# 320 columns of room and a start on 256 bytes for the tiles that move through TensorE

## The chip, the core and the metric

One NeuronCore of a Trainium2 chip runs the whole program. The metric is device microseconds from launch to end, the median of several runs. TensorE multiplies, VectorE (DVE), ScalarE (ACT) and GpSimd (POOL) do the elementwise work, SyncE (SP) issues the DMAs that bring weights from HBM.

## What is computed

One inference step of a two-layer decoder over 256 prompt tokens and 8 x 4 sample tokens, 288 tokens in all, model width 2048, feed-forward width 5632, float32. Cut to what matters:

```python
def trunk(x, ...):
    for l in range(2):
        h = rmsnorm(x, norm_mix[l])
        if l % 2 == 0:  y_tok, q_mem, ... = delta_mixer(h, ...)  # h @ w_in_delta, conv, gated delta rule
        else:           y_tok, q_mem, ... = pool_mixer(h, ...)   # h @ w_in_pool, windowed means, grouped w
        y_mem = cross_attn(q_mem, mem_k[l], mem_v[l])            # keys, values: rmsnorm(mem) @ w_mem_kv
        x = x + concat([y_tok, y_mem]) @ w_out[l]
        x = x + (silu(gate) * up) @ w_down[l]                    # gate, up = rmsnorm(x) @ w_gate_up[l]
    return rmsnorm(x, norm_final), states...
```

## The kernel before

Activations lie feature-major: a tile holds 128 features of all 288 tokens, 288 float32 columns or 1,152 bytes of each partition. Nearly all of the arithmetic is in the projections, and all projections go through one generator, `gemm_steps` (lines 143 to 166). It takes up to four 128-column blocks of a weight matrix, gives each block j a PSUM bank (`acc`), and walks the contraction in steps of `ks` blocks of 128 rows (two of them where four blocks are computed at once). For each step `wchunk` (line 103) fetches the weights by one DMA into one of three `wraw` tiles and splits them in two halves: ScalarE rounds them to float32r (`whi`, line 118) and VectorE takes the remainder (`wlo`, line 119). The activations have been split in the same way by `split` (line 168) into a hi tile and a lo tile. For each row block k and each column block j three matmuls follow, here called a triple:

```python
nc.tensor.matmul(pv, wh, xh, start=st, stop=False)      # line 161
nc.tensor.matmul(pv, wh, xl, start=False, stop=False)   # line 162
nc.tensor.matmul(pv, wl, xh, start=False, stop=en)      # line 163
```

The weight half is the stationary operand (128 x 128), the activation half is the moving operand (128 x 288). There are 5,860 triples in the program. Within one step j runs inside k, so four triples in a row, 12 matmuls, move the same pair of activation tiles; the last step of a projection runs k inside j.

The moving tiles come from three rotating sets. `at()` (line 65) gives one of `NA = 47` tiles named `a`, which serve all projections except two kinds; `bt()` (line 1350) gives tiles named `b` to the feed-forward stages (60 and 50 of them), which hold the hidden blocks that `w_down` multiplies, but for the first seven of each half, whose pairs are `a` tiles (line 1367); `dk()` (line 1448) gives 12 tiles to the small grouped product of the pooling mixer (36 triples).

Where these tiles lie follows from the order of the pools. At the bottom of each partition 16,384 bytes are set aside for descriptors of DMAs generated by software (the program constructor's default). Then come the constants, the pool `small` (line 50), the pool `act` with the 47 `a` tiles, the pool `wts` with `wraw`, `whi` and `wlo`, and the stage pools. The layout of the program before has:

- first `a` tile at byte 34,944 = 136 x 256 + 128, one every 1,152 = 4.5 x 256 bytes
- `whi` and `wlo` tiles at multiples of 2,048 bytes from byte 101,376 = 396 x 256; their 128-column slices at multiples of 512 bytes from there
- first `b` tile of the second feed-forward stage at byte 136,192 = 532 x 256, one every 1,152 bytes; the first stage's likewise on a multiple of 256
- first `dk` tile at byte 152,736 = 596 x 256 + 160, one every 1,152 bytes

So `a` and `b` tiles lie in turn on a multiple of 256 bytes and 128 bytes past one. Which of the two a hi or lo tile gets is decided by the rotation. The 16 pairs of the first feed-forward stage's input (`n1`), which all 22 of its gate and up projections move in the same order, lie as follows for row blocks 6 to 13 (start of hi, start of lo, each modulo 256):

```
k       6      7      8        9        10      11     12      13
hi, lo  0, 0   0, 0   128,128  128,128  128,0   0, 0   0,128   128,128
```

The order of the instructions on TensorE is fixed when the program is built. In the delta stage (some 100 to 800 us) the projections of the next heads are interleaved with the small matmuls of the delta rule, in the pooling stage with the cross attention; in the feed-forward stages there is nothing but triples.

Of the kernel before, what the change touches and what calls it, by code (L numbers as in the profile page):

```python
# [8 lines left out]
F32 = mybir.dt.float32  # L9
# [13 lines left out]
NT = NP + NS  # L23
NS3 = 3 * NS
# [18 lines left out]
def body(ctx: ExitStack, tc: tile.TileContext, i: dict, o: dict):  # L43
# [21 lines left out]
    def at(dt=F32):  # L65
        return apool.tile([P, NT], dt, name="a", tag="a", bufs=NA)

# [35 lines left out]
    def wchunk(pieces, nk, ncols, early=300):  # L103
        """Rows of weights, split into float32r parts: [(hi, lo)] of each 128 rows."""
        raw = wpool.tile([P, 1024], F32, name="wraw", tag="wraw", bufs=3)
        rv = raw[:, : nk * ncols].rearrange("p (k c) -> p k c", c=ncols)
        for ap, c0, w in pieces:
            nc.sync.dma_start(rv[:, :, c0 : c0 + w], ap)
        r = []
        step = 512 // ncols  # L110
        for k in range(0, nk, step):
            m = min(step, nk - k)
            n = m * ncols
            hi = wpool.tile([P, 512], F32R, name="whi", tag="whi", bufs=4)
            lo = wpool.tile([P, 512], F32R, name="wlo", tag="wlo", bufs=4)
            src = raw[:, k * ncols : k * ncols + n]
            with tc.high_priority(offset=early):
                nc.scalar.copy(hi[:, :n], src)  # L118
                nc.vector.tensor_tensor(  # L119
                    lo[:, :n], src, hi[:, :n].bitcast(F32), op=ALU.subtract  # L120
                )
            r += [
                (hi[:, j * ncols : (j + 1) * ncols], lo[:, j * ncols : (j + 1) * ncols])
                for j in range(m)
            ]
        return r
# [16 lines left out]
    def gemm_steps(w2d, cols, kt, act, on_block, ks=2, order=None, bank=None):  # L143
        """cols: [(first column, width)]; act(k) -> (hi, lo); on_block(j, psum)."""
        ncols = sum(w for _, w in cols)
        nb = ncols // P
        src = wsrc(w2d, cols)
        pss = [(bank or acc)() for _ in range(nb)]
        order = order or list(range(0, kt, ks))
        for k0 in order:  # L150
            nk = min(ks, kt - k0)
            w = wchunk(src(k0, nk), nk, ncols)
            last = k0 == order[-1]
            kj = [(k, j) for k in range(nk) for j in range(nb)]
            for k, j in sorted(kj, key=lambda t: t[1]) if last else kj:
                pv = pss[j][:, :NT]
                xh, xl = act(k0 + k)
                wh, wl = (t[:, j * P : (j + 1) * P] for t in w[k])
                st = k0 == order[0] and k == 0
                en = last and k == nk - 1  # L160
                nc.tensor.matmul(pv, wh, xh, start=st, stop=False)  # L161
                nc.tensor.matmul(pv, wh, xl, start=False, stop=False)  # L162
                nc.tensor.matmul(pv, wl, xh, start=False, stop=en)  # L163
                if en:
                    on_block(j, pv)
            yield
# [14 lines left out]
    class Norm:  # L181
        """Feature-major activations: hi/lo parts of x*w and the token sums of x^2."""
# [34 lines left out]
    def token_rstd(ss):  # L217
        """ss[token, tile]: sums of squares -> 1 / rms, [P, 3]."""
        v = small(3, "fv")
        nc.gpsimd.memset(v, 1.0)  # L220
        for r, c in ((slice(0, P), slice(0, 2)), (slice(0, NS), slice(2, 3))):
            nc.vector.tensor_scalar(v[r, c], ss[r, c], 1.0 / D, EPS, op0=ALU.mult, op1=ALU.add)
        return rsqrt(v, 3, "c3")

    def spread(r):
        """[token, tile] -> the same row of tokens on all partitions."""
        ps = aux()
        for t in range(3):
            rows = P if t < 2 else NS
            nc.tensor.matmul(  # L230
                ps[:, t * P : t * P + rows], r[:rows, t : t + 1].broadcast_to([rows, P]),
                ident[:rows, :rows], start=True, stop=True,
            )
        row = sp.tile([P, NT], F32, name="rrow", tag="rrow", bufs=1)
        nc.vector.tensor_copy(row, ps[:, :NT])
        return row

# [81 lines left out]
    with tc.tile_pool(name="mem", bufs=1) as mp:  # L319
# [50 lines left out]
        # masks: partition index j, free index c  # L370
# [18 lines left out]
        # sample tokens stand three times on the partitions: the parts of a split  # L389
        # product are then summed along one contraction  # L390
# [6 lines left out]
        # additive masks: 0 where the decay is kept, NEG elsewhere  # L397
# [4 lines left out]
        # within 32-blocks, [(block, j), c]: identity, and masks of the solved size s:  # L402
        # j in an even run of s, c in the odd run that follows
# [18 lines left out]
        # products with the states of the samples come out as rows (head, b, w|q, t)  # L422
# [17 lines left out]
        # 1 on the rows w, 0 on the rows q  # L440
# [27 lines left out]
    def attention(l, ys, g2, s4):  # L468
# [38 lines left out]
        # sample tokens: the four heads take a column tile each; a sequence's queries  # L507
        # (probabilities) stand in their own columns of a tile that is zero elsewhere
# [96 lines left out]
    W0 = i["w_in_delta"][0]  # L605
    y = [None] * 16
    with tc.tile_pool(name="delta", bufs=1) as dp:
# [4 lines left out]
        g2 = tiles("g", 2)       # 2 KB  # L612
        g1 = tiles("h", 6)       # 1 KB, keys of a unit
        gh = tiles("q", 3)       # 0.5 KB, sample tokens
        gp = tiles("u", 8)       # 2 KB, from the keys to the values of a unit
        v2 = tiles("v2", 4)      # 2 KB, values of a unit
        v1 = tiles("v1", 5)      # 1 KB, values of a unit
        ga = tiles("ag", 2)      # 2 KB, attention
        s4 = tiles("s", 4)       # 4 KB, recurrent states, cached keys and values
        pair = lambda shape, name: dp.tile(shape, F32, name=name, tag=name, bufs=2)  # L620

# [13 lines left out]
        def rates(ps):  # L635
# [24 lines left out]
            # softplus(a) = max(a, 0) + 2 atanh(e / (2 + e))  # L660
# [13 lines left out]
            # sigmoid(b) = max(e, b >= 0) / (1 + e)  # L674
# [6 lines left out]
        def decays():  # L681
            # cumulative decay within each chunk, and chunk totals
# [34 lines left out]
        # 24 columns: every fourth 128 rows in a column tile, summed with the transposition  # L717
# [16 lines left out]
        def decay(h0):  # L734
            """exp(gc_c - gc_j) for c >= j, heads h0, h0+1: [j, head, c]."""
# [50 lines left out]
        def project(fs):  # L786
            """Feature blocks of q | k | v (0..35: causal convolution and silu) and of
            z (36..47: silu), the z blocks last."""
# [83 lines left out]
        class Unit:  # L872
            """Gated delta rule for heads h0, h0+1: two prompt chunks of 128 and
            the sample tokens (8 sequences of 4)."""
# [4 lines left out]
            def bc(self, a, n=P):  # L879
                # [token, (chunk and) head], spread over head_dim  # L880
                return a.unsqueeze(len(a.shape)).broadcast_to(list(a.shape) + [P])

            def keys(self):
                # L = diag(r beta) K K' diag(r) with r = 1 / |k|, K as it comes from the
                # convolution: inverse(I + L) = diag(r beta) T diag(1 / (r beta)) with
                # T = inverse(I + K K' diag(r^2 beta) * decay); the scales of the rows
                # meet the vectors, and 1 / |q| the outputs
# [48 lines left out]
                # [j, head, (-L | attn), i]  # L936
# [43 lines left out]
                # U = transpose of inverse(I + L), by doubling the solved block; within  # L980
                # 32-blocks packed as [(block, j), chunk and head, i], samples last
# [19 lines left out]
                for s in (2, 4, 8, 16):  # L1001
# [13 lines left out]
                    # a sequence of samples is solved with the second size  # L1015
# [24 lines left out]
                # pairs of solved 32-blocks  # L1040
# [28 lines left out]
                # the two solved 64-blocks  # L1069
# [25 lines left out]
                # -w_k (feature-major)  # L1095
# [30 lines left out]
            def values(self):  # L1126
# [30 lines left out]
                # sample tokens: both products with each sequence's own state  # L1157
# [48 lines left out]
                # outputs, token-major, before the scale of q  # L1206
# [37 lines left out]
                # states  # L1244
# [77 lines left out]
    def out_proj(l, order, residual, after, ys=None):  # L1322
        """x = residual + y @ w_out; residual(g) adds to the 4 blocks of a group."""
# [24 lines left out]
    def ffn(l, nrm, fp, nbuf, after):  # L1348
        rs = None
        bt = lambda dt=F32: fp.tile([P, NT], dt, name="b", tag="b", bufs=nbuf)  # L1350
# [71 lines left out]
    W1 = i["w_in_pool"][0]  # L1422
    with tc.tile_pool(name="mix1", bufs=1) as qp:
# [4 lines left out]
        g2 = tiles("g", 6)       # 2 KB  # L1428
        ga = tiles("ag", 3)      # 2 KB, attention
        s4 = tiles("s", 5)       # 4 KB  # L1430
# [17 lines left out]
        dk = lambda: qp.tile([P, NT], F32R, name="dk", tag="dk", bufs=12)  # L1448
# [204 lines left out]
```

## Time and profile before

| what | value |
|---|---|
| median of 3 runs | 2762.17 us (2761.73 to 2766.06) |
| profiled execution, first to last instruction | 2763.6 us |
| TensorE busy with matmuls | 2720.2 us, 98% |
| VectorE, ScalarE, GpSimd busy | 58%, 46%, 12% |
| DMA engines busy (mean of 16) | 53%, 163 GB/s |
| mean granted TensorE clock | 0.995 |

The profile gives the span of the profiled execution alone; it lies 1.4 us above the median of the runs and within their spread. Matmuls are pipelined: one lasts some 295 ns from start to end in the records, and the next starts some 132 ns after it started. The number that counts is therefore the distance from start to start, not the duration.

### The profile page before, as it was taken

How to read it: one execution, taken by the hardware profiler on the slowest of the kernel's cores; microseconds unless marked ns; L12 is line 12 of the kernel's file. 1: busy time of each engine (PE TensorE's matmuls, PEld its weight loads, DVE VectorE, ACT ScalarE, POOL GpSimd, SP SyncE). 2: the span in 40 equal slices, each digit the busy share in tenths (PEclk: the TensorE clock that was granted, in tenths of full speed). 3: DMA queues.
4: the chain of work that ended last, by engine and by line, in shares of the span. 5: the costliest groups of instructions: out<-in, count | busy, mean ns of one | idle time of the engine just before them, and what ended most of it. 6: DMA issues, size and time to landing. Idle time of an engine off the chain costs nothing.

```text
span 2763.6 us, 55822 instructions
## 1 busy us (share of the span) xinstructions
PE 2720.2 (98%) x21808; PEld 2613.9 (95%) x21808; DVE 1606.1 (58%) x3240; ACT 1278.9 (46%) x2487; POOL 322.9 (12%) x671
## 2 busy tenths in 40 slices
PE   8999999999999999999999999999999999999998
PEld 6898888888999999999999988899999999999997
DVE  6657877686555554445555566766555544555544
ACT  6444545344544444344444455455444433444444
POOL 1103222231110010000010110111001000001000
PEclk9999999999999999999999999999999999999999
DMA  6544355635555555555555555655555555555554
GB/s 208 176 140 123 100 155 171 180 109 154 163 161 168 166 163 167 167 166 164 168 168 162 167 189 159 229 166 161 167 164 166 168 167 164 166 168 168 164 158 133
DMA packets 282954, 450.88 MB, mean 163 GB/s; under 512 B 18475, under 2 KB 104216, under 8 KB 282642
## 3 DMA queue, kind: packets, MB, share of 16 engines
q1 hardware_dynamic: 282690, 447.32, 52.4%
q8 instruction: 171, 2.80, 0.4%
q14 instruction: 93, 0.76, 0.1%
HBM read 434.93 MB, written 12.86 MB: 162 GB/s over the span
## 4 chain that ended last, share of the span: by engine, by line
PE 91%; DVE 3%; DMA 1%; ACT 1%; issue 1%; POOL 0%; SPq 0%; POOLq 0%; ACTq 0%; DVEq 0%
PE acc L161 27%; PE acc L163 27%; PE acc L162 27%; DVE wlo L119 1%; DMA s<-in_cache_mem_k_dram 1%; PE acc L273 1%; PE acc L274 1%; PE acc L275 1%; PE aux L523 0%; DMA memn<-in_mem_prompt_dram 0%; PE aux L569 0%; ACT whi L118 0%; PE aux L945 0%; PE aux L1011 0%; PE aux L745 0%
## 5 line engine op out<-in xcount | busy, mean ns | idle before, releaser
L119 DVE TENSOR_TENSOR wlo<-wraw,whi 128x512 fp32r<-128x512 f32 (+1 forms) x1548 | 1064.9, 694 | 996.9 <-ACT whi L118 968.6
L118 ACT CAST whi<-wraw 128x512 fp32r<-128x512 f32 (+1 forms) x1548 | 942.6, 616 | 1207.7 <-PE acc L162 1129.5
L161 PE MATMUL acc<-a,whi 128*128 128x288 f32 x4864 | 1444.6, 297 | 0.1
L163 PE MATMUL acc<-a,wlo 128*128 128x288 f32 x4864 | 1440.3, 296 | 0.9 <-DVE wlo L119 0.9
L162 PE MATMUL acc<-a,whi 128*128 128x288 f32 x4864 | 1441.2, 296 | 0.0
L162 PEld LDWEIGHTS acc<-a,whi 128*128 128x128 f32 x4864 | 916.0, 188 | 5.4 <-issue 2.9
L163 PEld LDWEIGHTS acc<-a,wlo 128*128 128x128 f32 x4864 | 914.5, 188 | 6.2 <-issue 2.4
L161 PEld LDWEIGHTS acc<-a,whi 128*128 128x128 f32 x4864 | 914.5, 188 | 5.3 <-issue 1.7
L161 PE MATMUL acc<-b,whi 128*128 128x288 f32 x960 | 283.7, 295 | 0.0
L163 PE MATMUL acc<-b,wlo 128*128 128x288 f32 x960 | 283.0, 295 | 0.0
L162 PE MATMUL acc<-b,whi 128*128 128x288 f32 x960 | 282.8, 295 | 0.0
L1362 POOL TENSOR_TENSOR b<-b,rrow 128x288 f32<-128x288 f32 x88 | 89.8, 1041 | 1266.9 <-ACT b L1361 1266.9
L162 PEld LDWEIGHTS acc<-b,whi 128*128 128x128 f32 x960 | 180.9, 188 | 0.0
L163 PEld LDWEIGHTS acc<-b,wlo 128*128 128x128 f32 x960 | 180.5, 188 | 0.0
L161 PEld LDWEIGHTS acc<-b,whi 128*128 128x128 f32 x960 | 180.4, 188 | 0.0
L196 POOL TENSOR_TENSOR ssum<-ssum,sq 128x288 f32<-128x288 f32 x60 | 56.4, 940 | 477.4 <-ACT sq L195 474.9
L275 PE MATMUL acc<-wlo,a 128*128 128x512 f32 x128 | 51.9, 405 | 0.0
L273 PE MATMUL acc<-whi,a 128*128 128x512 f32 x128 | 50.2, 414 | 1.4 <-ACT whi L118 1.1
L1360 DVE TENSOR_TENSOR b<-acc,rrow 128x288 f32<-128x288 f32 x88 | 40.1, 456 | 16.2 <-PE acc L163 16.1
L1361 ACT ACTIVATE b<-b 128x288 f32<-128x288 f32 x88 | 36.7, 441 | 26.2 <-DVE b L1360 25.9
L1366 DVE TENSOR_TENSOR b<-acc,b 128x288 f32<-128x288 f32 x88 | 40.0, 455 | 2.1 <-issue 0.3
L831 DVE SCALAR_TENSOR_TENSOR ckq<-xp,col_conv,ckq 128x312 f32<-128x312 f32 x72 | 37.4, 555 | 1.0 <-ACT ckq L829 0.9
(429 smaller groups left out, 1766.9 us busy)
## 6 DMA issues: line engine op xcount, KB each, us to landing
wraw<-in_w_gate_up_dram SPq DMA_DIRECT2D x352, 512.0 KB
wraw<-in_w_down_dram SPq DMA_DIRECT2D x176, 512.0 KB
wraw<-in_w_in_delta_dram SPq DMA_DIRECT2D x177, 256.0 KB
wraw<-in_w_out_dram SPq DMA_DIRECT2D x64, 512.0 KB
wraw<-in_w_mem_kv_dram SPq DMA_DIRECT2D x32, 512.0 KB
wraw<-in_w_in_pool_dram SPq DMA_DIRECT2D x32, 384.0 KB
wraw<-in_w_in_delta_dram SPq DMA_DIRECT2D x16, 512.0 KB
s<-in_cache_mem_k_dram SPq DMA_DIRECT2D x16, 512.0 KB
```

Source lines behind the costliest of these rows:

```text
L118: nc.scalar.copy(hi[:, :n], src)
L119: nc.vector.tensor_tensor(lo[:, :n], src, hi[:, :n].bitcast(F32), op=ALU.subtract)
L161: nc.tensor.matmul(pv, wh, xh, start=st, stop=False)
L162: nc.tensor.matmul(pv, wh, xl, start=False, stop=False)
L163: nc.tensor.matmul(pv, wl, xh, start=False, stop=en)
L196: nc.gpsimd.tensor_tensor(self.sum, self.sum, q, op=ALU.add)
L273: nc.tensor.matmul(pv, xh, w[k][0], start=st, stop=False)
L275: nc.tensor.matmul(pv, xh, w[k][1], start=False, stop=en)
L831: nc.vector.scalar_tensor_tensor(c[:, :312], xp[:, q : q + 312], convw(q, f), c[:, :312], op0=ALU.mult, op1=ALU.add,)
L1360: nc.vector.tensor_tensor(t, ps, rs, op=ALU.mult)
L1362: nc.gpsimd.tensor_tensor(t, t, rs, op=ALU.mult)
L1366: nc.vector.tensor_tensor(t, ps, t, op=ALU.mult)
```

## The change

The three sets of moving tiles get 320 columns (1,280 bytes) of room each, of which the first 288 are used; a tile of 32 columns (128 bytes) that nothing reads or writes is added to the pool `small`; the room at the bottom of the partition for software-generated DMA descriptors goes from 16,384 to 1,024 bytes. Comments and docstrings go as well. No instruction is added or removed by the text of the change, and each keeps its shape.

```diff
+NA_W = 320
     def at(dt=F32):
-        return apool.tile([P, NT], dt, name="a", tag="a", bufs=NA)
+        return apool.tile([P, NA_W], dt, name="a", tag="a", bufs=NA)[:, :NT]
+
+    sp.tile([P, 32], F32, name="fill")
...
-        bt = lambda dt=F32: fp.tile([P, NT], dt, name="b", tag="b", bufs=nbuf)
+        bt = lambda dt=F32: fp.tile([P, NA_W], dt, name="b", tag="b", bufs=nbuf)[:, :NT]
...
-        dk = lambda: qp.tile([P, NT], F32R, name="dk", tag="dk", bufs=12)
+        dk = lambda: qp.tile([P, NA_W], F32R, name="dk", tag="dk", bufs=12)[:, :NT]
...
-    nc = _bacc.Bacc("TRN2", target_bir_lowering=False, num_devices=1)
+    nc = _bacc.Bacc("TRN2", target_bir_lowering=False, num_devices=1, dynamic_dma_scratch_size=1024)
```

## Rows read from the trace of the kernel before

**Rows 1.** The page: span, and busy time of each engine.
```profile
span 2763.6 us, 55822 instructions
PE 2720.2 (98%) x21808; PEld 2613.9 (95%) x21808; DVE 1606.1 (58%) x3240; ACT 1278.9 (46%) x2487; POOL 322.9 (12%) x671
```

**Rows 2.** The page: chain that ended last, shares by engine.
```profile
PE 91%; DVE 3%; DMA 1%; ACT 1%; issue 1%; POOL 0%; SPq 0%; POOLq 0%; ACTq 0%; DVEq 0%
```

**Rows 3.** Windows, TensorE: stretch, its us, PE busy (matmuls), clock, DMA, GB/s.
```profile
0.00:60.00 60.00, 52.03 (x232) 1.00 0.67 226
60.00:200.00 140.00, 138.45 (x1262) 0.99 0.52 153
200.00:800.00 600.00, 584.11 (x5737) 0.99 0.48 146
800.00:1500.00 700.00, 700.00 (x5283) 1.00 0.54 166
1500.00:1960.00 460.00, 455.41 (x3332) 0.99 0.56 177
1960.00:2700.00 740.00, 739.98 (x5595) 1.00 0.54 166
2700.00:2763.60 63.60, 50.22 (x378) 0.91 0.41 129
```

**Rows 4.** Waits by engine: who waited for whom, us, times, longest.
```profile
ACT whi L118 <- PE acc L162: 1129.5, 1170, 6.1
DVE wlo L119 <- ACT whi L118: 968.6, 1113, 2.6
```

**Rows 5.** The page: costliest groups; line 163's matmuls, their idle time.
```profile
L163 PE MATMUL acc<-a,wlo 128*128 128x288 f32 x4864 | 1440.3, 296 | 0.9 <-DVE wlo L119 0.9
```

**Rows 6.** Line 161 alone: count, ns min/median/max, first and last start.
```profile
L161 PE MATMUL acc<-a,whi x4864: 288/294/802, 79.9 to 2726.5; 128*128 128x288 f32 x195
L161 PE MATMUL acc<-b,whi x960: 288/295/302, 1066.6 to 2747.2; 128*128 128x288 f32 x192
L161 PE MATMUL acc<-dk,whi x18: 292/298/401, 1726.1 to 1764.6; 128*128 128x288 f32 x18
L161 PE MATMUL aux<-dk,whi x18: 293/294/399, 1807.6 to 1814.6; 128*128 128x288 f32 x18
```

**Rows 7.** Timeline: first matmul of row block 6, of row block 14.
```profile
861.43 0.29 PE L161 MATMUL acc<-a,whi 128*128 128x288 f32 x1
...
874.17 0.29 PE L161 MATMUL acc<-a,whi 128*128 128x288 f32 x1
```

**Rows 8.** Windows, row blocks 6 to 13, 12 matmul starts in each; last: DMA.
```profile
861.43:863.01 1.58, 1.58 (x15) 1.00 0.69 253
863.01:864.59 1.58, 1.58 (x15) 1.00 0.29 57
864.59:866.19 1.60, 1.60 (x15) 1.00 0.72 271
866.19:867.79 1.60, 1.60 (x15) 1.00 0.26 76
867.79:869.37 1.58, 1.58 (x14) 1.00 0.67 255
869.37:870.95 1.58, 1.58 (x15) 1.00 0.33 66
870.95:872.57 1.62, 1.62 (x15) 1.00 0.68 259
872.57:874.17 1.60, 1.60 (x15) 1.00 0.43 79
```

**Rows 9.** The page: DMA queues, packets, MB, share of 16 engines.
```profile
q1 hardware_dynamic: 282690, 447.32, 52.4%
q8 instruction: 171, 2.80, 0.4%
q14 instruction: 93, 0.76, 0.1%
```

## The prediction

> **What bounds the kernel.** The first view to read is the list of busy times: TensorE is busy for 2720.2 of 2763.6 us, the next engine, VectorE, for 58% of the span [rows 1]. Then the chain that ended last: 91% of it is TensorE, and no other engine has more than 3% [rows 2]. Then the windows by stage, since an average over stages can hide a wait: in 800:1500 and 1960:2700, which are the feed-forward and output projections, TensorE is busy for 1439.98 of 1440 us at a granted clock of 1.00, its higher level of 2.4 GHz; what idle time it has lies in the delta stage (16 of 600 us), at both ends (8 and 13 us) and around the pooling mixer (5 us) [rows 3]. Last the waits: ScalarE waits 1129.5 us for matmuls to release `whi` tiles and VectorE waits 968.6 us for ScalarE [rows 4], while the matmuls of line 163 wait 0.9 us in all for `wlo` [rows 5]. So the weights are ready early and nothing but TensorE's own pace sets the end. There are 3 x 5,860 matmuls of 288 columns on lines 161 to 163, each line with the same counts [rows 6], and what counts of them is the distance from one start to the next.
>
> **Where the pace depends on the tiles' place.** The eight row blocks 6 to 13 of one gate projection follow each other without a gap, from the start at 861.43 to that at 874.17 us [rows 7]. Each is 12 matmuls of one pair of moving tiles, with the same shapes, the same code and weight slices on multiples of 512 bytes. (The windows count 14 or 15 because matmuls that are still running at an edge count too; 12 start in each.) Blocks 6, 7 and 11, with both tiles on a multiple of 256 bytes, take 1.58 us each. Blocks 8, 9 and 13, with both tiles 128 bytes past one, take 1.60 us each. The mixed pairs of blocks 10 and 12 take 1.58 and 1.62 us [rows 8]. The DMA share does not explain it: 1.58 us stands beside 253, 57 and 66 GB/s, and 1.60 us beside 271, 76 and 79 GB/s [rows 8]. All projections of this stage that move these pairs repeat these lengths within some 2 ns.
>
> To size it I took the starts of all triples in the timeline, from the first at 79.9 to the last at 2747.2 us [rows 6], took the time from the start of one triple to the start of what follows it, left out those of 430 ns and more (132 of the 5,667 that no other matmul cuts apart: waits, not pace), and sorted them by the places that the program's layout gives their hi and lo tile. Mean time of a triple:
> - both on a multiple of 256: 394.99 ns (1,068 triples of the program)
> - hi 128 past, lo on: 396.11 ns (1,808)
> - hi on, lo 128 past: 397.72 ns (1,648; the widest spread, as block 12 suggests)
> - both 128 past: 400.26 ns (1,300)
> - `dk` pairs, 32 and 160 past: some 400 ns (36)
>
> The standard error is below 0.2 ns in the four large classes. The order holds in each stage taken alone: in the first feed-forward stage 394.8 for both on against 400.3 for both past, in the second 395.0 against 400.3, in the delta stage 395.0 against 400.2. In the class of both on, no group by the places modulo 512 or 1024 has a mean more than 0.8 ns from the class's, so it is the class as a whole that should describe the new layout, where tiles lie 1,280 bytes apart.
>
> **The change, part by part.** *Room and place.* The descriptor space shrinks by 15,360 = 60 x 256 bytes and the added tile takes 128, so the first `a` tile moves to 34,944 - 15,360 + 128 = 19,712 = 77 x 256, and 1,280 = 5 x 256 keeps all 47 there. Their 47 x 1,280 bytes are 235 x 256, so `whi` and `wlo` stay on multiples of 256. The `b` tiles of the second stage begin at 136,192 - 15,360 + 128 + 47 x 128 = 126,976 = 496 x 256; those of the first are likewise all on. The `dk` tiles begin at 160 past a multiple and then all lie there, so the 36 triples that move them gain nothing; at 5 ns each that is under 0.2 us either way. The sum is the step of each other class to the first: 1,808 x 1.11 = 2.0 us, 1,648 x 2.72 = 4.5 us and 1,300 x 5.27 = 6.9 us, together 13.4 us, or 0.5% of the span. *What of it reaches the end.* In the two stretches where TensorE is never idle the same sum over the 3,610 triples there gives 8.6 us, all on the path. The other 4.8 us lie where TensorE is idle now and then (the idle time of [rows 3]); its order is fixed, so a triple that ends early brings the next instruction early, unless that one waits for a vector result anyway. I take nine tenths of these, 4.3 us. Total 12.9 us.
>
> *Who is late next.* One step of 24 matmuls gets 20 to 40 ns shorter out of 3.2 us. The splits that feed it wait for TensorE themselves [rows 4], so they follow; DMA engines at 54% of their time [rows 3] need 0.5% more. No new wait comes in. *The rest* costs nothing: no instruction is added, the splits and the vector work write the same 288 columns, the added tile has no user. The smaller descriptor space would matter only to DMAs whose descriptors software writes; 99% of the traffic is on the hardware-dynamic queue, the rest fetches instructions [rows 9].
>
> *Bounds.* The least is what the saturated stretches give if the rest is lost: 8.6 us, and half of it if the tiles' transitions in the new order cost something that the class doesn't show: 4 to 5 us. The most: the shortest of the 12-matmul blocks in which both tiles are on lasts 1.576 us against a median of 1.580; if all came down to that, 0.33 ns on each of 17,580 matmuls, it is 5.9 us more, some 19 us.
>
> [...] The rows show 12 matmuls of 288 columns in 1.58 to 1.62 us, 131.7 to 135 ns from start to start, at clock 1.00 [rows 8]. [...]
>
> **The rivals.** *Place is not the cause (chance 0.11), 2762 us.* The class may go with something else that alternates with it, such as which tile was written last, and the new layout would leave that as it is. For it: one mixed class is not halfway between the pure ones (396.1 where halfway is 397.6) and the other spreads widely. Against it: the pure classes agree to 0.2 ns between stages with quite different writers and tile sets (`a` alone, `a` and `b`).
>
> *The start is off by 128 (chance 0.04), slower.* The room keeps all tiles at one residue; which one, the sum of everything below them decides. If the added tile doesn't count with exactly 128 bytes, all `a` tiles lie 128 past, and the classes say 1,068 x 5.27 + 1,808 x 4.15 + 1,648 x 2.54 = 17.3 us more: 2779 us. It decides at one point, the residue of the first `a` tile. Against it: 128 needs no rounding, since the listed places of the small tiles show that they are rounded to 32 bytes.
>
> *The descriptors do need the room (chance 0.02), slower.* Then transfers would queue and steps would wait for their 512 KB; a step's 512 KB have to land every 3.2 us, so if room for one transfer at a time made each turn 5% longer than that, the two saturated stretches (1440 us) would grow by 5%, 72 us: 2834 us. The queue's kind [rows 9] speaks against it.
>
> **How the numbers follow.** Forecast, chance 0.83: 2763.6 - 12.9 = 2750.7 us for a profiled execution, and with the 1.4 us by which that lies above the median of the runs 2749.3 us. Its own bounds are 2743.5 (19 us less) and 2758 (4 us less). The range of 2743.5 to 2757 holds nearly all of it and nothing of the rivals, so about 8 in 10. A measurement of this kernel can tell some 0.2%, 5.5 us, from no change: below 2756.6 us it is faster. That is nearly the whole of the forecast (0.82), the same is the first rival with the forecast's edge (0.12), slower the two others (0.06).
>
> **What the profile after would show.** Row blocks of four column blocks last 1.58 us throughout the feed-forward stages, none 1.60 or 1.62. In 700 us of a saturated stretch some 5,315 matmuls are counted instead of 5,283 [rows 3]. TensorE's busy time falls by some 12 us and stays 98% of the span; the waits for `wlo` stay near 1 us. Blocks of 1.60 us everywhere would mean the wrong residue. Lengths as mixed as before would mean that place is not the cause. Blocks of 1.58 us with a span that hardly moves would mean that the gain turned into waits in the delta and pooling stages.

## The result and the profile after

The changed kernel takes 2750.65 us (median of 4 runs, 2749.05 to 2752.95) against 2761.95 us (4 runs, 2761.35 to 2766.06) of the kernel before: ratio 0.9949, 95% interval 0.9935 to 0.9962. The forecast was 2749.3 us. The profiled execution spans 2748.9 us, 14.7 us less than the one before [rows 1].

The page of the changed kernel: span and busy times, then the group of the lo matmuls (their line is 165 now, two below its place before), and two lines of the waits.

```profile
span 2748.9 us, 55822 instructions
...
PE 2705.1 (98%) x21808; PEld 2598.8 (95%) x21808; DVE 1606.8 (58%) x3240; ACT 1275.6 (46%) x2487; POOL 322.4 (12%) x671
...
L165 PE MATMUL acc<-a,wlo 128*128 128x288 f32 x4864 | 1437.4, 296 | 1.0 <-DVE wlo L121 0.9
```

```profile
ACT whi L120 <- PE acc L164: 1122.7, 1173, 7.2
DVE wlo L121 <- ACT whi L120: 970.7, 1124, 2.6
```

TensorE's busy time and that of its weight loads have fallen by 15.1 us, nobody else's has changed by more than 3.3 us, the count of instructions is the same, and the wait for `wlo` is still 0.9 us [rows 1, 4, 5]. The duration of one matmul has hardly moved (296 ns); the gain is in the distance between starts, which the windows show. Stretch, its length, TensorE's busy time and matmuls counted, clock, DMA share, GB/s:

```profile
200.00:800.00 600.00, 583.33 (x5763) 1.00 0.50 147
800.00:1500.00 700.00, 700.00 (x5319) 1.00 0.57 167
1500.00:1960.00 460.00, 455.53 (x3359) 1.00 0.56 178
1960.00:2700.00 740.00, 739.96 (x5622) 1.00 0.56 167
```

In 700 us 5,319 matmuls are counted instead of 5,283, in 740 us 5,622 instead of 5,595 [rows 3]. A sharper measure is the time from start to start over the same matmuls: the 5,317 that start in 800:1500 of the changed kernel take 700.07 us there and took 704.71 us before, the 5,620 of 1960:2700 take 740.00 us and took 743.56 us. Single blocks of 12 matmuls in a feed-forward stage, the same view:

```profile
855.17:856.75 1.58, 1.58 (x14) 1.00 0.83 302
856.75:858.33 1.58, 1.58 (x14) 1.00 0.32 45
858.33:859.91 1.58, 1.58 (x14) 1.00 0.77 287
```

Where blocks took 1.58, 1.60 and 1.62 us in turn [rows 8], all take 1.58 now; in the starts of the timeline thirteen in a row are 1,580 ns each to the nanosecond, although some of the tiles lie on a multiple of 512 bytes and the others 256 past one. Over the whole trace a triple takes 395.03 ns (those under 430 ns, 5,512 of them), and the four combinations of the places of hi and lo modulo 512 differ by 0.04 ns; the `dk` triples take 399.5 ns.

### The profile page after: what moved, and what is told of

Its sections match the earlier page's. It is cut to its first block, busy times and chain, and to the rows that moved or that the text cites. A ratio compares the mean times of both kernels' runs of the same rounds, so it can differ in the third digit from the quotient of the medians.

```text
span 2748.9 us, 55822 instructions
## 1 busy us (share of the span) xinstructions
PE 2705.1 (98%) x21808; PEld 2598.8 (95%) x21808; DVE 1606.8 (58%) x3240; ACT 1275.6 (46%) x2487; POOL 322.4 (12%) x671
## 3 DMA queue, kind: packets, MB, share of 16 engines
q1 hardware_dynamic: 282690, 447.32, 54.2%
## 4 chain that ended last, share of the span: by engine, by line
PE 91%; DVE 4%; ACT 1%; DMA 1%; issue 1%; POOL 0%; POOLq 0%; SPq 0%; ACTq 0%; DVEq 0%
PE acc L163 27%; PE acc L164 27%; PE acc L165 27%; DVE wlo L121 1%; PE acc L275 1%; PE acc L277 1%; PE acc L276 1%; PE aux L525 1%; PE aux L571 0%; PE aux L947 0%; PE aux L1013 0%; ACT whi L120 0%; PE aux L538 0%; DMA s<-in_cache_mem_k_dram 0%; PE aux L747 0%
```

## Experiments

So the time fits. Does the reason? The forecast's theory, P, is that the residue of the moving tile modulo 256 sets the pace. In the kernel before, all weight slices lie on multiples of 256, so "the moving tile lies on a multiple" and "the moving tile has the residue of the weights" can't be told apart there. The second is theory R. Theory N is what is left of the forecast's first rival now that the time has fallen: not place, but something that goes with even spacing. Three kernels tell them apart, and a fourth takes the descriptor space by itself. All have 1,024 bytes of descriptor space and all but the last 320 columns of room; each was timed beside the kernel before. In what follows a triple's mean is over those under 430 ns, as in the forecast.

**Without the added tile** everything above the `small` pool moves down by 128 bytes, weights too.

```diff
-    sp.tile([P, 32], F32, name="fill")
```

> The changed kernel without its added tile: room of 320 columns, but a and b tiles, and the weight halves too, all begin 128 bytes past a multiple of 256. Theory P (the residue of the moving tile modulo 256 alone sets the pace): every triple like the class of before with both tiles past, 400.3 ns, so 17 us over the kernel before, some 2779 us. Theory R (moving and stationary tile are quick when they have the same residue): 395 ns, some 2750 us. Theory N (place is not the cause, the even spacing of the tiles is): 395 ns, some 2750 us.

Measured: 2753.89 us, ratio 0.9960 (0.9945 to 0.9975), triple 395.03 ns. P falls: all moving tiles lie 128 past a multiple and the kernel is as quick as the changed one.

```profile
800.00:1500.00 700.00, 700.00 (x5319) 1.00 0.57 167
1960.00:2700.00 740.00, 739.94 (x5622) 1.00 0.57 166
```

The first count is that of the changed kernel to the matmul.

**Moving tiles 128 past, weights on multiples.** The added tile goes, 128 unused bytes come in between `wraw` and `whi` (`wfill` takes a tile of 32 columns from the pool on its first call) and 128 ahead of the `b` tiles of both feed-forward stages.

```diff
-    sp.tile([P, 32], F32, name="fill")
...
-        raw = wpool.tile([P, 1024], F32, name="wraw", tag="wraw", bufs=3)
+        raw = wpool.tile([P, 1024], F32, name="wraw", tag="wraw", bufs=3); wfill()
...
     with tc.tile_pool(name="ffn0", bufs=1) as fp:
+        fp.tile([P, 32], F32, name="bfill")
```

> Room of 320 columns, a and b tiles all 128 bytes past a multiple of 256, the weight halves on multiples of 256. P: 400.3 ns a triple, some 2779 us. R: 400.3 ns as well, the residues differ: some 2779 us. N: some 2750 us.

Measured: 2782.76 us, ratio 1.0066 (1.0049 to 1.0083), triple 399.99 ns.

```profile
800.00:1500.00 700.00, 700.00 (x5252) 1.00 0.57 165
1960.00:2700.00 740.00, 740.00 (x5553) 1.00 0.56 164
```

67 matmuls fewer in the same 700 us than in the kernel without the added tile, with `a` and `b` tiles at the same residue and only the weight halves moved. N falls.

**Weights 128 past, moving tiles on multiples.** The changed kernel with `wfill` and `bfill` as above, and the added tile kept.

> The changed kernel with the weight halves 128 bytes past a multiple of 256; a and b tiles stay on multiples. P: 395.0 ns a triple, some 2750 us, as the changed kernel. R: 400.3 ns, some 2779 us. N: some 2750 us.

Measured: 2779.51 us, ratio 1.0052 (1.0037 to 1.0067), triple 400.00 ns.

```profile
800.00:1500.00 700.00, 700.00 (x5252) 1.00 0.57 165
1960.00:2700.00 740.00, 740.00 (x5552) 1.00 0.56 165
```

Every moving tile lies on a multiple of 256 bytes, as the change wants it, and the kernel is slower than the one before. R alone expected all three.

**The descriptor space alone**, in the kernel before.

```diff
-    nc = _bacc.Bacc("TRN2", target_bir_lowering=False, num_devices=1)
+    nc = _bacc.Bacc("TRN2", target_bir_lowering=False, num_devices=1, dynamic_dma_scratch_size=1024)
```

> The kernel before with 1,024 instead of 16,384 bytes of descriptor space and nothing else: all tiles move down by 60 x 256 bytes and keep their residues. P, R and N: 2762 us, within 0.1% of the kernel before, with the four classes at 395.0, 396.1, 397.7 and 400.3 ns. If the descriptor space did part of the gain (or cost), up to 11 us less (or more).

Measured: 2764.41 us, ratio 1.0000 (0.9990 to 1.0009); the classes are 394.95, 396.12, 397.73 and 400.27 ns.

```profile
800.00:1500.00 700.00, 700.00 (x5284) 1.00 0.57 166
```

The space has no part in the gain; it only makes the room.

The same 5,317 matmuls as above, from start to start, in all six kernels:

| kernel | moving tile's place less the weights', modulo 256 | us |
|---|---|---|
| changed | 0 | 700.07 |
| without the added tile | 0 | 700.07 |
| moving tiles 128 past | 128 | 708.93 |
| weights 128 past | 128 | 708.93 |
| before | 0 and 128, mixed | 704.71 |
| before, small descriptor space | 0 and 128, mixed | 704.72 |

Where the places differ by the same amount the times agree to 0.01 us, although the executions as wholes differ (2748.9 and 2751.1 us for the first two): in this stretch nothing that changes from one execution to the next has a part in the pace.

**Which differences are quick?** From here on "difference" is the place of the moving tile less that of its weight slice, modulo 256. Two scans shift the pairs of activation tiles inside their room, from pair to pair: `offset` gives 0, 4, 8 ... 32 columns in turn, and `at` and `bt` return their tile from that column on.

```diff
-        hi = at(F32R) if hi is None else hi
-        lo = at(F32R) if lo is None else lo
+        f = offset() if hi is None else 0; hi = at(F32R, f) if hi is None else hi
+        lo = at(F32R, f) if lo is None else lo
```

> The changed kernel with the activation pairs of one projection input after another shifted inside their room by 0, 16, 32 ... 128 bytes, nine shifts in turn, hi and lo alike; weight halves on multiples of 256. P is out; what is asked is over which difference of places R holds. R-point (only equal residues are quick): 395.0 ns a triple at shift 0 and 400 ns at all eight others, some 2776 us. R-slope (the cost grows with the distance): values between 395 and 400 ns in order of the shift, some 2764 us. R-other (some difference is quicker than 0, which would beat the changed kernel): a class below 394 ns.

> The same nine shifts with the weight halves 128 bytes past a multiple of 256, so the moving tile lies 128, 112, 96 ... 0 bytes below the weights modulo 256. R-point: 395.0 ns only at shift 128, 400 ns at the others, some 2776 us. R-slope: falling from 400 to 395 ns with the shift, some 2764 us. R-other: a class below 394 ns. If the sign of the difference doesn't matter, the curve mirrors the one of the scan upwards.

Measured: 2766.54 and 2762.46 us (one run each; the kernel before 2767.25 us beside them). Triples by difference, ns, in the scan up: 0: 394.6, 16: 395.1, 32: 400.7, 48: 397.1, 64: 395.7, 80: 394.9, 96: 395.9, 112: 402.4, 128: 399.9; in the scan down, with the weights 128 bytes past: 128: 399.2, 144: 391.0, 160: 398.9, 176: 394.2, 192: 398.5, 208: 399.8, 224: 399.5, 240: 395.7, 0: 395.3. R-point and R-slope are out: there is no order in it, and equal residues are not the best. The dip at 144 was R-other's. That the difference alone counts, wherever the weights lie, is shown for 0 and 128 by these kernels and for 160 by the `dk` tiles (399.5 ns with the weights on multiples, 398.9 ns in the scan down); every other difference was measured with the weights at one place.

**Lo weights alone 128 past**, moving tiles and hi weights on multiples (`wfill` ahead of `wlo` instead of `whi`, with `bfill`).

> The changed kernel with the lo weight halves alone 128 bytes past a multiple of 256; hi halves and moving tiles on multiples. R-next (a matmul is slowed by the weights loaded for the matmul after it while it streams): the distance from line 162's start to line 163's is 1.7 to 5 ns longer than the other two, the triple 396.7 to 400 ns, 2760 to 2779 us. R-own (slowed by its own weights): the distance from line 163's start to the next line 161's is the long one. P, N: 395.0 ns, 2750 us.

Measured: 2748.47 us (one run; the kernel before 2767.25 us beside it), triple 393.48 ns, quicker than with all at one residue (395.03 ns), which neither side expected. The distances between the starts of lines 161, 162, 163 and 161 are 131.9, 133.3 and 128.3 ns on average.

```profile
800.00:1500.00 700.00, 700.00 (x5341) 1.00 0.57 168
1960.00:2700.00 740.00, 739.91 (x5644) 1.00 0.56 167
```

The middle distance equals that of the uniform kernel with difference 128 (400.0 / 3), and it is the matmul during which the shifted weights are loaded (in the trace line 163's weight load starts 3 ns after line 162's matmul), which speaks for R-next. But the third is shorter than either uniform pace (131.7 and 133.3), which neither R-next nor R-own gives. The mixed pairs of the kernel before show that a matmul's neighbours count as well: with all weights at one residue, hi 128 past and lo on, the three distances are 134.5, 129.7 and 131.9 ns, so the same difference 128 has 134.5 ns on line 161 and 131.9 ns on line 163. Which weight load a moving tile meets is not settled by this.

**Difference 144 throughout.** Weights 128 past (`wfill` and `bfill` as above), moving tiles 16.

```diff
-        return apool.tile([P, NA_W], dt, name="a", tag="a", bufs=NA)[:, :NT]
+        return apool.tile([P, NA_W], dt, name="a", tag="a", bufs=NA)[:, 4 : 4 + NT]
...
-        bt = lambda dt=F32: fp.tile([P, NA_W], dt, name="b", tag="b", bufs=nbuf)[:, :NT]
+        bt = lambda dt=F32: fp.tile([P, NA_W], dt, name="b", tag="b", bufs=nbuf)[:, 4 : 4 + NT]
```

> The changed kernel with the weight halves 128 bytes past a multiple of 256 and every a and b tile used from its fifth column on, 16 bytes past one: the moving tile lies 144 bytes above the weights modulo 256 throughout. The downward scan gave 391.0 ns a triple for this difference among others. R-other (each difference has its own pace, whatever its neighbours in time): 391.0 ns, 5,860 x 4.0 ns less than the changed kernel, some 2727 us. R-mixed (the 391.0 ns come from the changes between differences in the scan): back to 395 to 400 ns, 2750 to 2779 us.

Measured: 2730.09 us (2728.74 to 2731.74), ratio 0.9875 (0.9859 to 0.9892): quicker than both kernels. Triple 390.44 ns. The two stretches, two single blocks, and the page:

```profile
800.00:1500.00 700.00, 700.00 (x5387) 1.00 0.57 169
1960.00:2700.00 740.00, 739.78 (x5691) 1.00 0.57 168
...
855.82:857.38 1.56, 1.56 (x14) 1.00 0.83 301
857.38:858.94 1.56, 1.56 (x14) 1.00 0.41 47
```

```profile
span 2728.2 us, 55822 instructions
...
PE 2681.5 (98%) x21808; PEld 2574.0 (94%) x21808; DVE 1607.2 (59%) x3240; ACT 1276.3 (47%) x2487; POOL 323.2 (12%) x671
```

Blocks of 1.56 us are 130.0 ns a matmul. The pace of a difference carries from the scan to a kernel of its own. It is 4.6 ns a triple better than the changed kernel, which on all 5,860 triples would be 27 us; the span is 20.7 us shorter. In the two saturated stretches it all arrives: their same matmuls, 3,637 triples, take 691.21 and 730.85 us, 18.0 us less than in the changed kernel, or 5.0 ns a triple. The other 2,223 triples, in stages where TensorE also waits for others [rows 3], give 2.6 us of some 10.

**Finer than a line.** A line here is 16 bytes, the step of the two scans. The same scans with shifts of single words: first 4 to 28 bytes around difference 144, then all 64 words, each shift kept for the two pairs of a step.

> As the downward scan, with shifts of 4, 8, 12 ... 28 bytes in place of 0 to 128, seven in turn: differences 132 to 156 modulo 256. If places count in lines of 16 bytes, shifts of 4 to 12 bytes go with each other, and those of 16 to 28 with the 391 ns at 144 of the scan. If single words count, each shift has a value of its own, and one may lie below 391 ns.

> The changed kernel with shifts of 0, 4, 8 ... 124 bytes inside the room, 32 in turn, each for two pairs in a row (the two row blocks of a step); weight halves on multiples of 256. Word theory (each difference in words has a pace of its own): values scattered between some 390 and 415 ns with no order, about 395 at 0 and 16, 400.7 at 32, 402 at 112. Line theory (only the 16-byte line counts, the scan's scatter comes from its neighbours): the four shifts of a line within 1 ns of each other.

> The same with the weight halves 128 bytes past a multiple of 256, differences 128 to 252. Word theory: near 391 ns at 144 and 156, 413 at 148, 394 at 176, and possibly a value below 390 elsewhere. Line theory: the four shifts of a line within 1 ns of each other, which the fine scan already speaks against.

Measured: 2783.17, 2771.21 and 2780.93 us (one run each; the kernel before 2764.31 us and twice 2762.45 us beside them). In the fine scan the differences 132 to 156 gave 403.5, 407.3, 398.5, 393.9, 413.1, 399.8 and 392.1 ns. The whole circle from the two word scans, mean ns of a triple (those under 450), row = line of 16 bytes, column = word in it:

```
difference   +0     +4     +8    +12
   0       395.0  401.0  402.9  393.8
  16       395.3  400.7  406.2  390.2
  32       400.5  404.3  394.5  390.7
  48       396.8  401.1  402.5  399.1
  64       395.6  404.7  400.0  394.1
  80       393.4  409.5  400.5  390.0
  96       394.9  408.8  401.0  399.2
 112       399.3  405.0  408.9  394.7
 128       400.0  403.8  407.6  399.6
 144       393.4  413.7  400.4  390.8
 160       399.6  407.7  393.6  390.1
 176       394.3  409.0  399.8  390.8
 192       399.6  407.3  400.8  390.4
 208       400.2  408.0  403.6  394.1
 224       399.9  402.4  407.1  399.5
 240       395.7  406.7  397.9  389.8
```

The first eight rows have the weights on multiples of 256, the last eight 128 past. A mean's standard error is 0.1 to 0.8 ns. The line theory falls: words of one line lie up to 23 ns apart. The means follow no order that the table shows but one: those of one word past a line are all slow (400.7 to 413.7 ns). Eight words reach 389.8 to 390.8 ns, and nothing goes clearly below 390, which is 130 ns a matmul. A scan's figures still hold something of the neighbours: 144 has 391.0, 393.9 and 393.4 ns in three scans and 390.4 alone.

**Difference 84 throughout**, to see the other end.

```diff
-        return apool.tile([P, NA_W], dt, name="a", tag="a", bufs=NA)[:, :NT]
+        return apool.tile([P, NA_W], dt, name="a", tag="a", bufs=NA)[:, 21 : 21 + NT]
```

The `b` tiles likewise.

> The changed kernel with every a and b tile used from its 22nd column on, so that the moving tiles lie 84 bytes above the weights modulo 256 throughout, the slowest of the differences of the upward word scan but for its spread (409.5 ns a triple). Word theory (a difference has its own pace, alone as in the scan): 5,860 x 14.5 ns over the changed kernel's 395.05, some 2835 us, slower than the kernel before by 2.6%. If the scan's values come from neighbours: 395 to 400 ns, 2750 to 2779 us.

Measured: 2828.06 us (one run; the kernel before 2765.43 us beside it), triple 409.90 ns.

```profile
800.00:1500.00 700.00, 700.00 (x5124) 1.00 0.55 161
1960.00:2700.00 740.00, 739.92 (x5413) 1.00 0.55 161
```

The triple is what the scan gave. The time is 7 us under the expectation: the matmuls of the two saturated stretches take 726.66 and 767.61 us, 54.2 us over the changed kernel, as 14.9 ns on 3,637 triples make, but the other 2,223 triples add only 23.2 us of some 33. Nothing but the column from which the tiles are used lies between 2828 us and the changed kernel.

## Why the prediction was right, and where its reason was not

**The bound held.** TensorE is busy for 98% of the span before and after; its pace set the time in every experiment, most plainly in the two saturated stretches, and the splits followed it, as the forecast's "who is late next" said: in the quickest kernel VectorE is at 59%.

**The size held.** The forecast's class of both tiles on a multiple had 394.99 ns and stands for the whole kernel now, at 395.03. From 397.29 ns over all undisturbed triples before to 395.05 after it is 2.24 ns x 5,860 = 13.1 us, against 13.4 us in the sum. The same matmuls of the two saturated stretches take 4.64 and 3.56 us less, 8.2 us where 8.6 were worked out, so the term that is all on the path was sized well. The rest of the span fell by 6.5 us, where nine tenths of the remaining triples were to give 4.3. That part is not settled by one execution of each kernel: the first of the 5,317 matmuls starts at 802.72 us in the kernel before and at 806.93 us in the one with the descriptor space alone, whose tiles have the same residues. By the medians, which differ by 11.3 us, 3.1 us are left for it. That the total came within 1.4 us of the forecast is therefore luck in so far as it hangs on the nine tenths. The 5,315 matmuls in 700 us came out as 5,319, and the `dk` tiles gained nothing, as worked out.

**The reason was half of it.** The step that fails is "where the pace depends on the tiles' place": it took the residue of the moving tile for the cause, because the weights had one residue throughout and gave no contrast. The runs put in its place the difference between moving tile and weights: with every moving tile 128 past a multiple a triple takes 395.03 ns where the weights are 128 past too and 399.99 ns where they are not, and with every moving tile on a multiple 395.03 and 400.00 ns. The forecast did say that `whi` and `wlo` stay on multiples of 256, and thereby kept the one condition that its number needed, but as a side remark.

**The rivals.** *Place is not the cause*: out, by the result itself, since it gave 2762 us, and in the form of theory N by the kernel with moving tiles 128 past. *The start is off by 128*, at 2779 us: as written, without the added tile's 128 bytes, it is wrong, because the weights move along (2753.89 us); its price was right for the case in which they do not, 400.0 ns and ratio 1.0066, some 18 us where 17.3 were worked out. *The descriptors need the room*: out, ratio 1.0000.

**Weight loads beside running matmuls.** With the moving tiles at one residue, moving the weights by 128 bytes took the same 5,317 matmuls from 700.07 to 708.93 us, 1.3%; between differences 144 and 84 it is 5% (691.21 and 726.66 us). The Trainium skill's page "TensorE: Matmul & The Clock Gate", section "Step-by-step: what each phase is for", says that loading the next tile's weights takes no SBUF read bandwidth from the running matmul. If that were all, the place of the weights could hardly matter to the pace, and here it does. That the two reads meet in the memory is a reading of mine and not shown: what is shown is the dependence on the difference of their places.

**What stays open.** Why a given difference has its pace; whether the weights that a matmul meets are its own or the next one's, and how its neighbours enter, by which the mixed pairs of the kernel before lie where they do (396.1 and 397.7 ns); whether the differences other than 0, 128 and 160 keep their pace when the weights lie elsewhere; and whether a kernel with unlike differences for hi and lo could go below 390 ns, as single distances of 128.3 ns hint. None of it was tried further.

## What to carry to other kernels

Three things follow from this kernel and were not tried on another. When a stretch is nothing but back-to-back matmuls with a weight load each, compare the start-to-start distance of identical matmuls that differ in their tiles' places; a spread of a per cent there was bought back here by moving tiles, with no instruction added. What to set is the place of the moving tiles relative to the weights, so shift one against the other (a slice that starts some columns into a wider tile is enough) and scan, since here neither "aligned" nor "equal residues" is the best place. And a factor that never varies in a trace can't be seen in it: before naming a cause, ask what all its samples have in common.

## What was not expected of the hardware

At a granted clock of 1.00 (2.4 GHz), 128 x 128 weights and 288 float32r columns per matmul, the distance from start to start (a third of the mean triple) ran from 130.1 ns (difference 144 bytes modulo 256) over 131.7 (0) and 133.3 (128) to 136.6 ns (84), in kernels with one difference throughout. A shift by a single word, 4 bytes, changed the mean triple by up to 20 ns in the scans (393.4 at 144, 413.7 at 148). Two kernels whose tiles and weights lie elsewhere, but with the same difference of 0 or of 128, spend the same time on 5,317 matmuls to 0.01 us.
